# Ten products of a tuned decoder kernel moved from VectorE to GpSimd, six of them behind a ScalarE copy out of PSUM

## The chip, the cores and the metric

The kernel runs on one core of a Trainium2 chip. The metric is the device time of one execution in microseconds. The kernel before took 2746.87 us (median of 3 runs, 2746.59 to 2746.87). The engines are TensorE (PE in the profile), its weight loads (PEld), VectorE (DVE), ScalarE (ACT), GpSimd (POOL) and SyncE (SP), which here only issues loads.

## What is computed

The reference is a decoder trunk of two layers on 512 positions of width 2048: a pooling mixer (layer 0) and a gated linear recurrence (layer 1), each followed by a gated input embedding. The change lies in the first steps of layer 0:

```python
h = rmsnorm(x, g_pre[0])               # x * rsqrt(mean(x*x) + eps) * g
uz = jnp.einsum('bsd,de->bse', h, w_in[0])
u, z = uz[..., :D_INNER], uz[..., D_INNER:]
```

The product has 8192 output channels, 64 tiles of 128 channels by 512 positions. Tiles 0 to 31 are u, tiles 32 to 63 are z. All arithmetic is fp32.

## The kernel before

Activations lie with channels on the partitions and positions along the free axis, so a tile is 128x512. Each fp32 operand is split into a rounded part `hi` and a rest `lo`, and a product is three matmuls, hi by hi, hi by lo and lo by hi (`mm3`, lines 125 to 128). ScalarE makes `hi` and VectorE makes `lo`. For weights that is `chunk_of` (lines 100 to 123): SyncE loads a chunk into `raw`, ScalarE scales it by the gain into `hi` (L118), VectorE subtracts into `lo` (L119); `raw`, `hi` and `lo` have two buffers each.

The norm's factor for each position, `R`, is not known when the first product starts. So the product is taken of the raw x, and each result tile is multiplied by `R` afterwards. The order of the work is:

1. `first_unit` (line 228, written out by hand) makes tiles 0 to 3 of the product while x is still being loaded, and gathers the squares of x. It has four PSUM banks.
2. `raw_copies` (line 295) has ScalarE copy these four banks to SBUF (tiles zs0 to zs3). `norm.finish` (line 188) makes `R` in SBUF: ScalarE's square root, VectorE's reciprocal.
3. Lines 648 to 650: VectorE multiplies each of the four tiles by `R` in place (L649), and `keep` (line 336) stores it to DRAM, by a DMA that GpSimd's queue issues (L338). The stored u is read back much later, by `pool_in` (line 429).
4. Line 651: `unit` (line 130) makes tiles 4 to 9, with six PSUM banks of the eight, from 16 chunks. A chunk holds one of the 16 tiles of x's channels and 6 weight tiles: 18 matmuls of 512 columns.
5. Lines 652 to 659: `mix` and `renew` prepare sums and differences of x for the steps that follow; nearly all of it is VectorE's, with ScalarE's `hi` halves (L149) and VectorE's `lo` halves (L150) of `split`. `mix` also multiplies x by `R` (L347).
6. Lines 660 to 664: VectorE multiplies each of the six banks by `R` into an SBUF tile `u` (L663), and `keep` stores it. The tiles take turns in the tags D and F, two buffers each, so the fifth reuses the first's and the sixth the second's, once they are stored.
7. Lines 665 to 668: `pair_unit` (line 397) makes the other tiles, two at a time, with four banks, from four pair chunks (`pair_chunk`, line 368). A pair chunk needs on VectorE four sums of 128x256 (L384 to L387), the `lo` of three weight blocks (L388, 128x768) and two `lo` of sums (L150), and on ScalarE the `hi` of L382 and two of L149. With its weights TensorE does 42 matmuls of 256 columns (L410 to L412). The sums of even pair chunks are split into the slots zs0 to zs3. The finished pair leaves PSUM by VectorE (L415 to L422), and `keep` stores it.

Outside `first_unit` and the tail, the framework orders the instructions of each engine when the kernel is built, by priority and by its own estimate of when things are ready. What lies in `urgent()` has high priority: the chunks, the copies of `raw_copies`, and L663. At run time each engine goes through its queue in order, so an instruction that waits holds up what is behind it. GpSimd's queue holds the stores of `keep` in the order of their tiles, with little else between 2 us and the pools.

Of the kernel before, what the change touches and what calls it, by code (L numbers as in the profile page):

```python
# [10 lines left out]
ALU = mybir.AluOpType  # L11
# [31 lines left out]
def trunk(ctx: ExitStack, tc: tile.TileContext, order, xT, pT, wst, par, out):  # L43

    nc = tc.nc
    V, A, G, T = nc.vector, nc.scalar, nc.gpsimd, nc.tensor
# [8 lines left out]
    def bank(name):  # L55
        return ps.tile([P, S], F32, tag="bank", name=name)
# [3 lines left out]
    def tmp(tag, name):  # L60
        return work.tile([P, S], F32, tag=tag, name=name, bufs=BUFS[tag])

    def urgent(now=True):
        return tc.high_priority() if now else nullcontext()
# [65 lines left out]
    def unit(kind, layer, xs, kts, ets, trickle=False, gain=True):  # L130


        ne, nk = len(ets), len(kts)
        banks = [bank(f"{kind}_{e}") for e in range(ne)]
        per = CH // ne
        cuts = list(range(0, nk, per))
        for a, b in zip(cuts, cuts[1:] + [nk]):
            ks = range(a, b)
            hi, lo = ahead.pop(0) if ahead else chunk(kind, layer, [kts[k] for k in ks], ets, gain)
            steps = [(k, e) for e in range(ne) for k in ks]  # L140
            if trickle and ks[-1] < nk - 1:
                steps.sort()
            for k, e in steps:
                t = (k - a) * ne + e
                mm3(banks[e], hi[:, t, :], lo[:, t, :], *xs[k], k == 0, k == nk - 1)
        return banks
# [148 lines left out]
    def raw_copies(banks, tags):  # L295

        r = []
        for b, t in zip(banks, tags):
            c = slot(t, F32, "rawc")
            with urgent():  # L300
                A.copy(c, b)
            r.append(c)
        return r
# [32 lines left out]
    def keep(m, t):  # L336

        G.dma_start((U + Z)[m], t)  # L338
# [307 lines left out]
    b = raw_copies(b0, [f"zs{e}" for e in range(4)])  # L646
    R = norm.finish()
    for e in range(4):
        V.tensor_tensor(b[e], b[e], R, op=ALU.mult)  # L649
        keep(e, b[e])  # L650
    b = unit("w_in", 0, X, KX, range(4, 10))
    for kk in range(6):
# [7 lines left out]
    for e in range(6):  # L660
        t = tmp("DF"[e % 2], "u")
        with urgent():
            V.tensor_tensor(t, b[e], R, op=ALU.mult)  # L663
        keep(4 + e, t)
    for m in range(10, 60, 2):
        pair_unit(m)
# [2 lines left out]
    b = unit("w_in", 0, X, KX, range(60, 64), gain=False)  # L669
    ds = pool_in(0)  # L670
    zs = gate_in(0)
    for e in range(4):
        t = tmp("F", "z")
# [40 lines left out]
    for k in range(NK):  # L714
        t = es[k]
# [5 lines left out]
    b = unit("w_in", 1, X, KX, [0, 1, 2, 3, 32], trickle=True)  # L721
    b = raw_copies(b, ["c8", "c10", "c12", "c14", "zs0"])
    R = norm.finish()
# [6 lines left out]
    for n in range(1, NU):  # L730
        b = unit("w_in", 1, X, KX, range(4 * n, 4 * n + 4))
# [25 lines left out]
    b = [bank("w_ple_gate_h") for _ in range(2)]  # L757
# [9 lines left out]
    with tc.manual_schedule():  # L767
        b = [bank("w_ple_gate_h") for _ in range(2)]
# [38 lines left out]
        for k in range(8):  # L807
# [3 lines left out]
            b = held[k // 2]  # L811
# [68 lines left out]
```

## Time and profile before

| What | us |
|---|---|
| median of 3 runs | 2746.87 |
| the profiled execution, its own time | 2747.97 |
| its span, first to last instruction | 2746.3 |
| TensorE busy | 2734.5 |
| VectorE busy | 2007.7 |
| ScalarE busy | 1185.4 |
| GpSimd busy | 148.7 |

The span is 1.7 us shorter than the same execution's time. A matmul's end is modelled, and matmuls overlap, so TensorE's busy share tells only where it stood still. Times within the span count from its first instruction. In a timeline each line gives the start, the time taken, engine, line, operation, out<-in and the number of instructions merged in it, and in brackets the idle time before it and what ended that.

### The profile page before, as it was taken

To read this page: it belongs to the slowest core of one execution; us is meant where nothing else is said; L and a number is where in the kernel's file an instruction comes from. 1 tells how busy PE (TensorE), PEld (TensorE's weight loads), DVE (VectorE), ACT (ScalarE), POOL (GpSimd) and SP (SyncE) were. 2 spreads that over 40 slices of the span, in tenths; PEclk is the share of its full clock that TensorE was granted. 3 is DMA by queue.
4 is the path that set the end of the run, shared out by engine and by line. 5 is a ranking of instruction groups with operands and counts; after the bars stand their busy time and mean duration, and the time that the engine had idled before them with its cause. 6 is when DMAs were issued, how large, how long until landed. Compare 5 with 4: busy or idle time off the path is not lost.

```text
span 2746.3 us, 36706 instructions
## 1 busy us (share of the span) xinstructions
PE 2734.5 (100%) x14124; PEld 2350.5 (86%) x14124; DVE 2007.7 (73%) x3219; ACT 1185.4 (43%) x1731; POOL 148.7 (5%) x265
## 2 busy tenths in 40 slices
PE   9999999999999999999999999999999999999999
PEld 8899999998888888888888888888888888888887
DVE  6988888788848554577488876767686858598856
ACT  6444444444423222255365543434343434345554
POOL 0000000014303000000000000000000000000002
PEclk9999999999999999999999999999999999999999
DMA  5334434346534333333323233233233332332333
GB/s 179 124 124 136 134 127 135 124 142 219 161 115 142 119 112 104 115 117 95 104 85 107 92 100 99 93 100 97 96 100 93 99 97 95 100 101 92 96 94 117
DMA packets 98576, 314.57 MB, mean 115 GB/s; under 512 B 12000, under 2 KB 16224, under 8 KB 98400
## 3 DMA queue, kind: packets, MB, share of 16 engines
q1 hardware_dynamic: 84384, 271.58, 31.4%
q0 software_dynamic: 11200, 36.71, 3.9%
q10 hardware_dynamic: 2816, 3.94, 0.4%
q8 instruction: 110, 1.80, 0.3%
q14 instruction: 66, 0.54, 0.1%
HBM read 291.21 MB, written 20.97 MB: 114 GB/s over the span
## 4 chain that ended last, share of the span: by engine, by line
PE 98%; DVE 1%; DMA 0%; issue 0%; ACT 0%; ACTq 0%; DVEq 0%
PE w_in L128 10%; PE w_in L126 10%; PE w_in L127 10%; PE w_out L128 8%; PE w_out L126 8%; PE w_out L127 8%; PE w_in_s L412 6%; PE w_in_s L410 6%; PE w_in_s L411 6%; PE w_ple_gate L127 4%; PE w_ple_gate L128 4%; PE w_ple_gate L126 4%; PE pool_w L128 2%; PE pool_w L126 2%; PE pool_w L127 2%; PE w_in L264 2%
## 5 line engine op out<-in xcount | busy, mean ns | idle before, releaser
L119 DVE SCALAR_TENSOR_TENSOR lo<-raw,pr,hi 128x512 fp32r<-128x512 f32 (+5 forms) x424 | 290.5, 718 | 319.9 <-ACT hi L118 310.9
L118 ACT ACTIVATE hi<-raw,pr 128x512 fp32r<-128x512 f32 (+5 forms) x424 | 277.5, 696 | 449.4 <-PE w_in L127 273.6
L126 PE MATMUL w_in<-xhi,hi 128*128 128x512 f32 x1184 | 461.5, 390 | 0.0
L127 PE MATMUL w_in<-xlo,hi 128*128 128x512 f32 x1184 | 460.6, 389 | 0.0
L128 PE MATMUL w_in<-xhi,lo 128*128 128x512 f32 x1184 | 460.3, 389 | 0.0
L128 PE MATMUL w_out<-yhi,lo 128*128 128x512 f32 x1024 | 398.7, 389 | 0.0
L126 PE MATMUL w_out<-yhi,hi 128*128 128x512 f32 x1024 | 398.4, 389 | 0.0
L127 PE MATMUL w_out<-ylo,hi 128*128 128x512 f32 x1024 | 398.4, 389 | 0.0
L122 DVE TENSOR_TENSOR lo<-raw,hi 128x1024 fp32r<-128x1024 f32 (+2 forms) x194 | 234.2, 1207 | 213.4 <-ACT hi L121 207.6
L121 ACT ACTIVATE hi<-raw 128x1024 fp32r<-128x1024 f32 (+2 forms) x194 | 203.7, 1050 | 424.8 <-PE w_out L127 232.8
L126 PEld LDWEIGHTS w_in<-xhi,hi 128*128 128x128 f32 x1184 | 222.2, 188 | 46.8 <-ACT ig L512 0.3
L127 PEld LDWEIGHTS w_in<-xlo,hi 128*128 128x128 f32 x1184 | 222.2, 188 | 46.7 <-issue 0.5
L128 PEld LDWEIGHTS w_in<-xhi,lo 128*128 128x128 f32 x1184 | 222.2, 188 | 46.1 <-DVE lo L119 0.2
L128 PEld LDWEIGHTS w_out<-yhi,lo 128*128 128x128 f32 x1024 | 192.2, 188 | 40.9 <-DVE lo L122 1.0
L127 PEld LDWEIGHTS w_out<-ylo,hi 128*128 128x128 f32 x1024 | 192.2, 188 | 40.0
L126 PEld LDWEIGHTS w_out<-yhi,hi 128*128 128x128 f32 x1024 | 192.2, 188 | 39.7
L126 PE MATMUL w_ple_gate<-xhi,hi 128*128 128x512 f32 x480 | 187.4, 391 | 0.0
L128 PE MATMUL w_ple_gate<-xhi,lo 128*128 128x512 f32 x480 | 186.8, 389 | 0.0
L127 PE MATMUL w_ple_gate<-xlo,hi 128*128 128x512 f32 x480 | 186.7, 389 | 0.0
L315 DVE TENSOR_TENSOR o<-w_out,o 128x512 f32<-128x512 f32 x224 | 152.0, 684 | 33.2 <-PE w_out L128 31.4
L382 ACT ACTIVATE hi<-raw 128x768 fp32r<-128x768 f32 x100 | 84.7, 847 | 150.9 <-PE w_in_s L411 143.9
L149 ACT ACTIVATE s24hi<-s 128x512 fp32r<-128x512 f32 x100 | 63.2, 632 | 130.2 <-PE w_in_s L411 113.4
(283 smaller groups left out, 5525.5 us busy)
## 6 DMA issues: line engine op xcount, KB each, us to landing
raw<-in_w SPq DMA_DIRECT2D x420, 512.0 KB, 3.5
raw<-in_w SPq DMA_DIRECT2D x60, 384.0 KB, 3.0
raw<-in_w SPq DMA_DIRECT2D x48, 320.0 KB, 2.9
u<-u POOLq DMA_DIRECT2D x38, 256.0 KB, 3.5
zs<-z POOLq DMA_DIRECT2D x32, 256.0 KB, 4.0
z<-pair POOLq DMA_DIRECT2D x28, 256.0 KB, 3.0
u<-pair POOLq DMA_DIRECT2D x22, 256.0 KB, 3.0
raw<-in_w SPq DMA_DIRECT2D x17, 256.0 KB, 5.4
```

The lines of the kernel that those rows point to most:

```text
L118: A.activation(hi[:, sl, :], raw[:, sl, :], AF.Copy, scale=g)
L119: V.scalar_tensor_tensor(lo[:, sl, :], raw[:, sl, :], g, hi[:, sl, :].bitcast(F32), op0=ALU.mult, op1=ALU.subtract)
L121: A.activation(hi, raw, AF.Copy)
L122: V.tensor_tensor(lo, raw, hi.bitcast(F32), op=ALU.subtract)
L126: T.matmul(acc, hi, xhi, start=start, stop=False)
L127: T.matmul(acc, hi, xlo, start=False, stop=False)
L128: T.matmul(acc, lo, xhi, start=False, stop=stop)
L315: V.tensor_tensor(O[k], banks[e], O[k], op=ALU.add)
L382: A.activation(hi, flat[:, H:], AF.Copy)
L410: T.matmul(acc[p], hi, x[0][:, ts], start=kk == 0 and p in (1, 6, 3, 4), stop=False, skip_group_check=True)
L411: T.matmul(acc[p], hi, x[1][:, ts], start=False, stop=False, skip_group_check=True)
L412: T.matmul(acc[p], lo, x[0][:, ts], start=False, stop=kk == NK // 2 - 1, skip_group_check=True)
```

## The change

VectorE's products with `R` in lines 649 and 663 become GpSimd's. [...] Each product stands ahead of its own store, which GpSimd's queue issues too. The copy and the product of the six are both urgent; the first four products are not, as before.

```diff
@@ -646,7 +646,7 @@
     b = raw_copies(b0, [f"zs{e}" for e in range(4)])
     R = norm.finish()
     for e in range(4):
-        V.tensor_tensor(b[e], b[e], R, op=ALU.mult)
+        G.tensor_tensor(b[e], b[e], R, op=ALU.mult)
         keep(e, b[e])
     b = unit("w_in", 0, X, KX, range(4, 10))
     for kk in range(6):
@@ -660,7 +660,8 @@
     for e in range(6):
         t = tmp("DF"[e % 2], "u")
         with urgent():
-            V.tensor_tensor(t, b[e], R, op=ALU.mult)
+            A.copy(t, b[e])
+            G.tensor_tensor(t, t, R, op=ALU.mult)
         keep(4 + e, t)
     for m in range(10, 60, 2):
         pair_unit(m)
```

## Rows read from the trace of the kernel before

**Rows 1.** The page: busy time, share of the span and instructions of each engine.

```profile
PE 2734.5 (100%) x14124; PEld 2350.5 (86%) x14124; DVE 2007.7 (73%) x3219; ACT 1185.4 (43%) x1731; POOL 148.7 (5%) x265
```

**Rows 2.** Waits of TensorE over the span: us in total, times, longest.

```profile
PE w_in_s L412 <- DVE lo L388: 3.5, 1, 3.5
```

**Rows 3.** Timeline of TensorE, 117 to 130 us: start, us, engine, line, operation.

```profile
117.67 0.28 PE L410 MATMUL w_in_s<-xhi,hi 128*128 128x256 f32 x1
...
120.66 0.28 PE L411 MATMUL w_in_s<-t34lo,hi 128*128 128x256 f32 x1
124.39 0.39 PE L412 MATMUL w_in_s<-xhi,lo 128*128 128x256 f32 x1 [3.45 <-DVE lo L388]
...
125.57 0.36 PE L411 MATMUL w_in_s<-xlo,hi 128*128 128x256 f32 x1
...
129.11 0.28 PE L412 MATMUL w_in_s<-xhi,s24lo 128*128 128x256 f32 x1
129.23 0.28 PE L410 MATMUL w_in_s<-t12hi,s13hi 128*128 128x256 f32 x1
```

**Rows 4.** Stretches: length, busy PE, PEld, DVE, ACT, POOL, granted clock, DMA share, GB/s.

```profile
122.00:124.00 2.00, 0.00 (x0) 0.00 (x0) 2.00 (x5) 0.63 (x1) 1.08 (x2) 1.00 0.50 191
126.00:128.00 2.00, 2.00 (x11) 2.00 (x11) 2.00 (x5) 0.00 (x1) 0.00 (x0) 0.50 0.55 215
```

**Rows 5.** Timelines of VectorE and ScalarE, 113 to 125 us.

```profile
113.29 0.42 DVE L384 TENSOR_TENSOR s<-raw 128x256 f32<-128x256 f32 x1 [0.80 <-DMA raw<-in_w]
...
116.64 2.47 DVE L663 TENSOR_TENSOR u<-w_in,R_pre 128x512 f32<-128x512 f32 x4
...
121.14 1.33 DVE L663 TENSOR_TENSOR u<-w_in,R_pre 128x512 f32<-128x512 f32 x2 [1.02 <-DMA u<-u]
...
123.39 1.82 DVE L388 TENSOR_TENSOR lo<-raw,hi 128x768 fp32r<-128x768 f32 x2
...
117.69 0.85 ACT L382 ACTIVATE hi<-raw 128x768 fp32r<-128x768 f32 x1 [1.19 <-issue]
...
120.51 0.84 ACT L382 ACTIVATE hi<-raw 128x768 fp32r<-128x768 f32 x1
```

**Rows 6.** Timelines of VectorE and TensorE, 58 to 94 us.

```profile
58.40 2.49 DVE L649 TENSOR_TENSOR rawc<-rawc,R_pre 128x512 f32<-128x512 f32 x4
...
65.71 1.02 DVE L119 SCALAR_TENSOR_TENSOR lo<-raw,pr,hi 128x768 fp32r<-128x768 f32 x1
...
69.16 0.39 PE L128 MATMUL w_in<-xhi,lo 128*128 128x512 f32 x1
...
91.19 1.01 DVE L119 SCALAR_TENSOR_TENSOR lo<-raw,pr,hi 128x768 fp32r<-128x768 f32 x1
...
93.64 0.39 PE L128 MATMUL w_in<-xhi,lo 128*128 128x512 f32 x1
```

**Rows 7.** Stretches 58 to 113 and 113 to 125 us, columns as in rows 4.

```profile
58.00:113.00 55.00, 55.00 (x244) 45.53 (x244) 54.50 (x97) 28.52 (x43) 2.33 (x4) 1.00 0.38 116
113.00:125.00 12.00, 8.55 (x53) 7.52 (x52) 10.65 (x23) 5.88 (x9) 3.24 (x6) 1.00 0.59 215
```

**Rows 8.** Instructions of line 301: ns min/median/max, first and last start, forms.

```profile
L301 ACT COPY rawc<-w_in x9: 564/588/607, 51.6 to 1460.1; 128x512 f32<-128x512 f32 x9
```

**Rows 9.** Instructions of line 338, and us from issue to landing.

```profile
L338 POOL DMA_DIRECT2D u<-u x6: 539/539/544, 117.6 to 122.8; - x6
...
DMA to landing us min/median/max: 2.3/3.2/5.6
```

**Rows 10.** Timeline of GpSimd in the tail.

```profile
2735.96 4.84 POOL L780 TENSOR_TENSOR rawc<-rawc,o 128x256 f32<-128x256 f32 x7 [1.17 <-DVE rawc L777]
```

**Rows 11.** Instructions of lines 627 and 622, one of each beside GpSimd's sums of L780.

```profile
L627 DVE TENSOR_TENSOR nacc_out<-nacc_out,gsg x2: 426/708/989, 2717.1 to 2726.0; 128x256 f32<-128x256 f32 x2
...
L622 DVE TENSOR_TENSOR sq_last<-rawc x2: 424/626/828, 2718.4 to 2731.3; 128x256 f32<-128x256 f32 x2
```

**Rows 12.** Instructions of line 456, GpSimd's copies in the pools.

```profile
L456 POOL COPY s<-s x48: 183/661/3449, 652.5 to 887.5; 128x2 f32<-128x2 f32 x24, 128x4 f32<-128x4 f32 x16, 128x8 f32<-128x8 f32 x8
```

## The prediction

> **What bounds the kernel now.** I read the page's busy shares first: TensorE is busy 2734.5 us of the span [rows 1]. So the change can matter only where TensorE waits, and the view of who waited for whom, kept to TensorE, lists all of that. The line to see is the longest: one wait of 3.5 us, matmul L412 on VectorE's lo of L388 [rows 2]. The four others, each shorter, lie at the very start and end of the span, where this change does nothing. Between this wait and the tail there is none, so a changed order of later work has nothing to win there.
>
> Next I read what that one wait costs. The matmul before it started at 120.66, it started at 124.39, and such matmuls normally start 0.12 apart (129.11 and 129.23): 3.61 us lost [rows 3]. [...] From 125.57 to 129.11 there are 17 steps from start to start in 3.54 us, where 17 x 0.12 = 2.04 would do: 1.50 us lost. The hole costs 3.61 + 1.50 = 5.1 us, and that is all that can be gained here.
>
> Then why lo is late: VectorE's timeline. It prepares the first pair chunk from 113.29, then does four of the six products with R (L663, from 116.64), the sums of the next chunk, and stands 1.02 us in front of the fifth product, whose tile is still being stored. Only then comes the awaited lo, at 123.39 [rows 5]. The six products and the wait are 6 x 0.60 + 1.0 = 4.6 us right ahead of the late instruction. The change aims at a real hole.
>
> **The change part by part.**
>
> Removed from VectorE: ten products. Four take 2.47 us from 116.64 [rows 5] and four 2.49 from 58.40 [rows 6], about 0.6 each as they overlap: 10 x 0.60 = 6.0 us, and the 1.02 us wait. Between 58 and 113 us VectorE is busy 54.5 of 55.0 us [rows 7], so 2.4 us less there moves everything behind it forward; TensorE does not wait there, so nothing is gained from it directly. The 3.6 + 1.0 us at 116 to 121 are worth up to the whole hole.
>
> Added on ScalarE: six copies out of PSUM, 0.59 us each by the same form elsewhere (L301) [rows 8]: 3.5 us. In 113 to 125 us ScalarE is busy 5.9 of 12.0 us [rows 7], so they fit. The fifth and sixth copy reuse the tiles of the first and second, so on ScalarE's queue they stand in front of the next hi until those are stored. The pair's matmuls begin at 117.67 [rows 3], right behind the last chunk's 18, which are 0.227 apart (108 of them lie between the two matmuls of rows 6, 24.48 us); the first bank's three are the first of them, done near 114.5, and its copy ends near 115.1; a product (below) takes 1.4, the store's issue 0.54, its landing 3.2 to 5.6 [rows 9]: near 120.3 for the first, 1.9 later for the second, so ScalarE may stand until 122.2. Behind it waits the hi of the third pair chunk, at 120.51 before [rows 5]; at 123 with its lo by 125 it is still ahead of 127.7, when TensorE gets there (117.67 + 2 x 42 x 0.12). Cost nothing; if a store landed 3 us later it would begin to cost.
>
> Added on GpSimd: ten products of 128x512. No row has one. The nearest is the sum of two 128x256 tiles at the end: seven in 4.84 us, 0.69 apart [rows 10]. For twice the columns the bounds are 0.69 and 1.38; I take 1.38, as the work is per column. The six products and stores take turns in one queue: 6 x (1.38 + 0.54) = 11.5 us from 115, done by about 127; the first four by 67, the last landing near 70, while their tiles are next written after the sums of 113.29 [rows 5]. Nobody reads what is stored before the pools, which come after all pair units. So GpSimd being slower costs nothing by itself.
>
> What it does to VectorE is the term that decides. VectorE's 128x256 instructions with two inputs in SBUF run 0.43 us undisturbed and 0.99 (L627) and 0.83 (L622) beside GpSimd's sums, a loss of 0.56 and 0.40 [rows 11]. In return GpSimd's copies of two to eight columns, 0.18 us at their shortest, have a median of 0.66 us where VectorE is busy, and one took 3.4 [rows 12]. So each holds the other up. For a 128x512 product I take a loss to VectorE of 2 x 0.56 = 1.12 us; bounds 0 (the product always falls into a gap of VectorE's) and 1.38 (its whole length). Nearly all VectorE work here has two SBUF inputs, and without gaps in it the product always displaces something. [...]
>
> So each product frees 0.60 us of VectorE and takes about 1.12.
>
> First stretch: the four products put VectorE 4 x 1.12 = 4.5 us behind by about 67. What waits is TensorE, for lo (L119): the one started at 65.71, 1.02 long, is used at 69.16, a margin of 2.4 us; the tightest, at 91.19, is used at 93.64, a margin of 1.4 [rows 6]. TensorE stands 4.5 - 2.4 = 2.1 us (0 to 4.1 by the bounds). The 2.4 us that VectorE is relieved of lie behind this point and help later.
>
> Second stretch: the hi of the second chunk runs from 117.69 to 118.54 [rows 5], its lo could end by 119.5, and TensorE needs it at 117.67 + 42 x 0.12 = 122.7: a margin of 3.2 us. Four products fit in before that (1.92 each from 115): 4.5 - 3.2 = 1.3 us of standing (0 to 5.1, with all six at 1.38).
>
> Clock: the one hole inside the kernel lost 1.50 us to the slow clock after 3.6 us of idling. Two short holes may bring none or 1.50 each; I take 0.75 in all.
>
> Sum: -5.1 + 2.1 + 1.3 + 0.75 = -0.95 us. The profiled execution took 2747.97 us (span 2746.3), 1.1 above the median of 2746.87; the difference applies alike: 2746.87 - 0.95 = 2745.9 us. A measurement of this kernel can tell about 0.2%, 5.5 us, from no change.
>
> **The rivals.**
>
> 1. The hole closes and nothing opens: GpSimd's products find gaps, or VectorE's margins hold. For it: 1.4 to 3.2 us of margin, and the 2.4 us relieved. Against it: no gap in 58 to 113. It gives 2746.87 - 5.1 = 2741.8 us, just short of 0.2%. Anything further would need time that TensorE doesn't lose today.
>
> 2. Slower: VectorE is held for the full 1.38 us of every product, and each is met by the tightest margin. First stretch 4 x 1.38 - 1.4 = 4.1, second 6 x 1.38 - 3.2 = 5.1, slow clock twice 1.50: 12.2 - 5.1 = +7.1, 2754.0 us. It passes +5.5 from a hold of about 1.22 us (10 x 1.22 - 4.6 + 3.0 - 5.1). For it: the losses on L627 and L622 are near their maximum. [...]
>
> 3. ScalarE's fifth and sixth copy wait for stores that GpSimd issues late. With each of GpSimd's first two products delayed by 3.4 us, as its worst copy was, the second store lands near 129, the third chunk's lo ends near 131.4 where TensorE wants it at 127.7: 3.7 us and 1.50 of clock, -5.1 + 5.2, 2747.0 us. For it: the queue is in order. Against it: the median wait is far shorter.
>
> **How the numbers follow.** The forecast, a hole partly given back: 0.50. Rival 1: 0.28, of which 0.06 beyond -5.5 us. Rival 2: 0.15. Rival 3: 0.07. Faster 0.06, same 0.79, slower 0.15. The range runs from rival 1 with a little to spare, 2741.4, up towards rival 2, 2752.5, which leaves out most of it.
>
> **What would show it.** TensorE's wait on L388 near 121 should be gone or under 2 us. A wait on L119 between 65 and 95 shows the first stretch right; none shows the hold smaller than I took, or hidden. VectorE's 128x512 instructions of 0.68 us beside the products should show 1.2 to 2 us. If they don't, the term that decides is wrong, and rival 1 stands. GpSimd's products should start about 1.9 us apart. A long wait of ScalarE on a store means rival 3. If TensorE stands over 10 us between 58 and 140, rival 2 is right.

## The result, and the profile after

The changed kernel took 2765.9 us (median of 4 runs, 2763.47 to 2769.64) beside 2746.87 for the kernel before: 1.007 times as long, 95% interval 1.0057 to 1.0082. It is slower by 0.7%, outside the range I gave. The profiled execution took 2763.47 us with a span of 2761.7, 15.4 us longer than the span before.

TensorE's waits come first, as before. Waits of TensorE over the changed kernel's span (us in total, times, longest):

```profile
PE w_in_s L412 <- DVE s13lo L150: 3.8, 8, 1.0
PE w_in_s L410 <- ACT hi L382: 3.4, 1, 3.4
PE w_in L128 <- DVE lo L119: 2.8, 1, 2.8
...
PE w_in_s L412 <- DVE lo L388: 0.2, 1, 0.2
```

The old hole [rows 2] is gone: L388 is down to 0.2 us. Three things stand in its place. One is a wait on L119, as the first stretch forecast, one a wait on ScalarE's hi of L382, and one is a kind that no step of the prediction has: eight waits on s13lo, seven of them after 160 us, where TensorE never stood before. The stretches around the first two (columns as in rows 4) show a granted clock of 0.50 again behind each, as in the second line of [rows 4]:

```profile
64.00:66.00 2.00, 0.00 (x0) 0.00 (x0) 2.00 (x5) 1.21 (x3) 0.49 (x1) 1.00 0.70 260
...
68.00:70.00 2.00, 2.00 (x6) 1.51 (x6) 2.00 (x6) 0.63 (x1) 0.00 (x0) 0.50 0.35 138
...
126.00:128.00 2.00, 0.00 (x0) 0.00 (x0) 2.00 (x5) 0.09 (x1) 2.00 (x4) 1.00 0.15 55
...
132.00:134.00 2.00, 2.00 (x11) 2.00 (x11) 2.00 (x3) 0.00 (x0) 1.68 (x3) 0.50 0.84 328
```

VectorE is busy in all four, 2.00 of 2.00 us, so the question is with what. Timeline of VectorE in the changed kernel:

```profile
56.73 3.49 DVE L347 SCALAR_TENSOR_TENSOR x<-x,pr,R_pre 128x512 f32<-128x512 f32 x2
60.14 3.58 DVE L350 TENSOR_TENSOR t<-x 128x256 f32<-128x256 f32 x1
...
120.74 1.51 DVE L384 TENSOR_TENSOR s<-raw 128x256 f32<-128x256 f32 x1
122.18 0.41 DVE L387 TENSOR_TENSOR s<-raw 128x256 f32<-128x256 f32 x1
122.51 4.43 DVE L385 TENSOR_TENSOR s<-s,raw 128x256 f32<-128x256 f32 x1
...
130.18 1.50 DVE L384 TENSOR_TENSOR s<-raw 128x256 f32<-128x256 f32 x1
...
131.94 1.94 DVE L385 TENSOR_TENSOR s<-s,raw 128x256 f32<-128x256 f32 x1
```

All but the first row are 128x256 instructions, which take 0.42 us in [rows 5]; here one takes 4.43. Beside them, GpSimd's timeline of the same kernel:

```profile
56.06 3.62 POOL L649 TENSOR_TENSOR rawc<-rawc,R_pre 128x512 f32<-128x512 f32 x2 [54.30 <-DVE R_pre L196]
...
60.89 2.54 POOL L649 TENSOR_TENSOR rawc<-rawc,R_pre 128x512 f32<-128x512 f32 x2
...
120.38 1.59 POOL L664 TENSOR_TENSOR u<-u,R_pre 128x512 f32<-128x512 f32 x1 [55.89 <-ACT u L663]
...
122.87 3.78 POOL L664 TENSOR_TENSOR u<-u,R_pre 128x512 f32<-128x512 f32 x3
...
129.83 1.57 POOL L664 TENSOR_TENSOR u<-u,R_pre 128x512 f32<-128x512 f32 x1 [1.59 <-ACT u L663]
...
132.30 1.29 POOL L664 TENSOR_TENSOR u<-u,R_pre 128x512 f32<-128x512 f32 x1
```

Each long 128x256 instruction ends about 0.3 us after GpSimd's product or products do. L385 at 122.51 ends at 126.94, three products from 122.87 end at 126.65: VectorE got no turn between them. Why the planner put two and three products in a row, with the stores behind them, the runs do not show. Nor do the starts tell which engine came first: L350 at 60.14 and L385 at 122.51 begin 0.75 and 0.36 us before the products that hold them, and GpSimd's times in a profile are rough. What VectorE lost in all: L347 3.49 - 1.41 (the pair's time without a product, shown further down) = 2.1; L350 3.2; then 1.1, 4.0, 1.1 and 1.5. That is 13.0 us for ten products, 1.3 each.

Where the time went along the span can be read from one instruction that every pair unit has once, the first of its evacuation (L415: count, ns, first and last start). In the kernel before:

```profile
L415 DVE COPY pairs<-w_in_s x25: 412/417/425, 140.1 to 623.8; 128x256 f32<-128x256 f32 x25
```

and in the changed kernel:

```profile
L415 DVE COPY pairs<-w_in_s x25: 417/419/425, 147.8 to 637.7; 128x256 f32<-128x256 f32 x25
```

The first is 7.7 us later, the last 13.9: the 24 units between them take 489.9 us instead of 483.7, with no product of the change anywhere near. So there are two losses, and the second can't be the products' presence itself. The split is rough, because TensorE began the chunks of `unit` at 51.97 us in the one execution and at 50.30 in the other. By the starts of TensorE's own matmuls, the changed kernel loses 6.3 us from there to the second pair, and 9.2 from there to the end of the pair units.

What differs in the pair units is the order that the planner gave VectorE. In the kernel before, with the evacuation under way (timeline of VectorE):

```profile
365.76 0.41 DVE L417 TENSOR_TENSOR pairs<-pairs,w_in_s 128x256 f32<-128x256 f32 x1
366.09 0.68 DVE L150 TENSOR_TENSOR s13lo<-s,s13hi 128x512 fp32r<-128x512 f32 x1
366.69 0.41 DVE L418 TENSOR_TENSOR pairs<-pairs,w_in_s 128x256 f32<-128x256 f32 x1
```

and in the changed kernel, at the same place of a unit:

```profile
378.81 0.41 DVE L417 TENSOR_TENSOR pairs<-pairs,w_in_s 128x256 f32<-128x256 f32 x1
...
379.48 0.42 DVE L418 TENSOR_TENSOR pairs<-pairs,w_in_s 128x256 f32<-128x256 f32 x1
...
381.47 0.95 DVE L388 TENSOR_TENSOR lo<-raw,hi 128x768 fp32r<-128x768 f32 x1
382.34 0.42 DVE L422 TENSOR_TENSOR pair<-pairs,w_in_s 128x256 f32<-128x256 f32 x1
382.67 0.69 DVE L150 TENSOR_TENSOR s13lo<-s,s13hi 128x512 fp32r<-128x512 f32 x1
383.27 0.69 DVE L150 TENSOR_TENSOR s24lo<-s,s24hi 128x512 fp32r<-128x512 f32 x1
```

There, s13lo stands behind the first three of the evacuation's eight instructions (L415 to L417); here behind all of it, three sums (L386, L384 and L387, among the lines left out) and an L388. TensorE's timeline of the changed kernel shows what that costs in this unit:

```profile
383.41 0.38 PE L412 MATMUL w_in_s<-t12hi,s13lo 128*128 128x256 f32 x1 [1.05 <-DVE s13lo L150]
```

The view of waits lists only the longer ones. By the starts of the matmul records, a matmul on s13lo begins more than 0.17 us behind the one ahead of it, where 0.12 is usual, 18 times after 160 us in the changed kernel, 6.7 us in all, and never in the kernel before.

The order repeats: of the 25 units, 22 have the same early order in the kernel before, and 24 the same late one in the changed kernel. I call them the **early** and the **late order**.

### The profile page after: what moved, and what is told of

Read it like the earlier page. It is cut to its first block, busy times and chain, and to the rows that moved or that the text cites. A ratio compares the mean times of both kernels' runs of the same rounds, so it can differ in the third digit from the quotient of the medians.

```text
span 2761.7 us, 36691 instructions
## 1 busy us (share of the span) xinstructions
PE 2741.9 (99%) x14124; PEld 2352.8 (85%) x14124; DVE 2011.4 (73%) x3209; ACT 1183.9 (43%) x1737; POOL 162.5 (6%) x275
## 4 chain that ended last, share of the span: by engine, by line
PE 88%; DVE 6%; DMA 4%; issue 1%; ACT 0%; POOL 0%; DVEq 0%; ACTq 0%; POOLq 0%
PE w_in L128 9%; PE w_in L126 9%; PE w_in L127 9%; PE w_out L126 8%; PE w_out L128 8%; PE w_out L127 8%; PE w_ple_gate L128 4%; PE w_ple_gate L126 4%; PE w_ple_gate L127 4%; DMA raw<-in_w 4%; PE w_in_s L412 4%; PE w_in_s L411 3%; PE w_in_s L410 3%; PE pool_w L128 2%; PE pool_w L127 2%; PE pool_w L126 2%
## 5 line engine op out<-in xcount | busy, mean ns | idle before, releaser
L119 DVE SCALAR_TENSOR_TENSOR lo<-raw,pr,hi 128x512 fp32r<-128x512 f32 (+5 forms) x424 | 290.8, 719 | 319.5 <-ACT hi L118 310.6
L382 ACT ACTIVATE hi<-raw 128x768 fp32r<-128x768 f32 x100 | 84.6, 846 | 137.0 <-PE w_in_s L411 119.1
```

Source lines behind the costliest of these rows:

```text
L119: V.scalar_tensor_tensor(lo[:, sl, :], raw[:, sl, :], g, hi[:, sl, :].bitcast(F32), op0=ALU.mult, op1=ALU.subtract)
L382: A.activation(hi, flat[:, H:], AF.Copy)
```

## The experiments

Two theories for the later loss. A, which the second batch calls C: the planner's order of the pair units is a loss of its own. B: all of it follows from GpSimd's hold on VectorE. A third question, D, is what the hold itself is. Each batch of four ran beside its own runs of the kernel before, whose medians were 2750.25, 2749.18 and 2752.12 us, spread over 9.6 to 11 us; so the ratios with their intervals count. The two columns on the right are first and last start of L415 in the profiled execution.

| run | GpSimd's products | order | median, us | ratio to before, interval | first, last L415 |
|---|---|---|---|---|---|
| four | first 4 | late | 2762.13 | 1.0042 (1.0027 to 1.0057) | 141.0, 635.4 |
| six | last 6 | early | 2750.81 | 1.0002 (0.9993 to 1.0012) | 143.8, 629.2 |
| copy | none | late | 2757.93 | 1.0023 (1.0012 to 1.0033) | 138.8, 633.0 |
| half | 10, half width | early | 2750.79 | 0.9998 (0.9988 to 1.0008) | 142.0, 625.7 |
| before_tag | none | late | 2759.76 | 1.0032 (1.0020 to 1.0044) | 140.6, 635.9 |
| after_tag | 10 | early | 2754.79 | 1.0018 (1.0008 to 1.0028) | 147.8, 630.4 |
| copy_mix | none | early | 2748.53 | 0.9992 (0.9982 to 1.0001) | 139.5, 623.2 |
| copy_order | none | early | 2745.80 | 0.9985 (0.9976 to 0.9995) | 136.8, 622.0 |
| tag_set | 10 fills | early | 2743.00 | 0.9968 (0.9958 to 0.9978) | 135.0, 619.9 |
| tag_one | 10, one input | early | 2747.93 | 0.9987 (0.9977 to 0.9998) | 141.1, 621.2 |
| four_tag | first 4 | early | 2753.29 | 1.0005 (0.9994 to 1.0016) | 145.3, 628.7 |
| after_again | 10 | late | 2767.12 | 1.0060 (1.0036 to 1.0083) | 149.7, 642.0 |

### One part alone: four, six, copy, half

four: the kernel before with

```diff
     for e in range(4):
-        V.tensor_tensor(b[e], b[e], R, op=ALU.mult)
+        G.tensor_tensor(b[e], b[e], R, op=ALU.mult)
```

> Only the first four products on GpSimd; the six stay on VectorE, without a copy. Theory A (two separate costs: GpSimd's products hold VectorE for their whole length, and the planner's new order of the pair units, which comes with the six copies, loses about 10 us later): the order of the pair units is close to that of before, so only the first stretch is paid: VectorE instructions of about 3.5 us near 57 to 63, a wait of TensorE on L119 near 66 of about 2.8 us with its slow clock, the old hole on L388 still there, and no growth after 160 us. 2749 to 2753 us. Theory B (all 19 us follow from the hold, the later drift being VectorE's lag that is never made up): 4 of 10 products, some 2754 us, with small waits of TensorE on s13lo all through the pair units.

six: the kernel before with

```diff
         with urgent():
-            V.tensor_tensor(t, b[e], R, op=ALU.mult)
+            A.copy(t, b[e])
+            G.tensor_tensor(t, t, R, op=ALU.mult)
```

> Only the six products on GpSimd, behind their ScalarE copies; the first four stay on VectorE. Theory A: the pair units have the new order (TensorE's is the same as in the changed kernel), so the later drift of about 10 us is there, and the wait in the first stretch (2.8 us and its slow clock) is gone: 2760 to 2763 us. Theory B: 6 of 10 products, 2746.9 + 11 = 2758 us.

copy: the same, with `V.tensor_tensor(t, t, R, op=ALU.mult)` for the product.

> The six copies on ScalarE as in the change, but all ten products on VectorE, the six from the SBUF copy; no GpSimd product at all. Theory A: the pair units stand in nearly the order of the changed kernel, so the drift of about 10 us after 160 us is there without any hold, and TensorE waits on s13lo: 2752 to 2759 us. Theory B: no product on GpSimd, no hold, no drift: 2742 to 2748 us.

half: the changed kernel with both products on `[:, :S // 2]` of their tiles.

> The changed kernel with each GpSimd product on the first 256 of 512 columns; the other 256 columns of these ten tiles are left unscaled. TensorE's order is the same. If the hold is the length of the product, the long VectorE instructions shrink to about half (4.43 us for three products to about 2.4, 3.5 for two to about 2), and the waits of 2.8 us on L119 and 3.4 us on ScalarE's hi nearly go: about 6 to 8 us less than the changed kernel. Theory A: the drift after 160 us stays, 2757 to 2760 us. Theory B: the drift halves too, near 2756 us, with about 5 us of growth after 160. If the hold does not depend on length, the time stays at 2764 to 2766 us.

Three of the four missed both theories' numbers: four is far above, six far below, and half 5 us below the nearer one. I had tied the late order to the copies, and that was wrong. Read by the order that each kernel in fact got, the runs fall apart cleanly: in the late order the 24 steps of L415 take 494.4 us (four) and 494.2 (copy), in the early one 485.4 (six) and 483.7 (half). copy has no product on GpSimd and grows as much as four, which B can't have. half fits a hold that goes with the length of the product. Its GpSimd timeline shows two products of 256 columns in a row:

```profile
122.62 1.43 POOL L664 TENSOR_TENSOR u<-u,R_pre 128x256 f32<-128x256 f32 x2
```

and its VectorE timeline the instruction that they hold, 1.81 us, where three of 512 columns held one for 4.43, so 0.70 lost for each product instead of 1.34:

```profile
122.54 1.81 DVE L386 TENSOR_TENSOR s<-raw,s 128x256 f32<-128x256 f32 x1
```

half also has the early order, so its distance to the changed kernel, 0.7%, is not the hold's alone. The order had to be set apart.

### The order alone: before_tag, after_tag, copy_mix, copy_order

before_tag is the kernel before, after_tag the changed kernel, both with the same letter changed, the fifth tile's tag:

```diff
-        t = tmp("DF"[e % 2], "u")
+        t = tmp("DFDFFF"[e], "u")
```

> The kernel before with one letter changed: the fifth of the six tiles takes the tag F instead of D. All ten products stay on VectorE, no copies. The planner then settles on the other order of VectorE's work in 22 pair units, the one that the changed kernel has: the awaited lo of L388 and the sums of the next chunk stand ahead of the pair's evacuation, and two s13lo late. Theory C (the planner's order of the pair units is a loss of its own, about 0.4 to 0.5 us a unit, whatever led to it): TensorE waits on s13lo, growth of 8 to 13 us after 160 us, 2756 to 2762 us. Theory B (the later drift follows from GpSimd's hold): no hold, no drift, 2747 to 2752 us.

> The changed kernel with the same one letter: all ten products on GpSimd, copies as in the change. Here the letter sends the planner back to the order of the pair units of before. Theory C: the growth after 160 us falls to that of the runs in that order (2 to 6 us), while the waits near 66 and 130 us from GpSimd's products stay: 2750 to 2757 us, 9 to 15 below the changed kernel. Theory B: the ten holds are all there, so 2763 to 2769 us.

copy_mix is copy with

```diff
     mix(6)
+    renew(4)
     mix(7)
-    for kk in range(4, 8):
+    for kk in range(5, 8):
         renew(kk)
```

> Six copies on ScalarE, all ten products on VectorE, and one preparation step (renew(4)) moved ahead of mix(7), which sends the planner to the order of the pair units of before. Theory C: no hold, no late order, and the old hole on L388 closed (the copy kernel was 3.3 us ahead of before at 130 us): 2743 to 2749 us, below the kernel before by 1 to 5 us. Theory B has nothing to hold here either, but gave copy no drift, so it does not expect a gain over the 2757.9 us of copy.

copy_order is copy with

```diff
-    for e in range(6):
+    for e in (0, 1, 2, 5, 4, 3):
```

> As copy (six copies on ScalarE, all products on VectorE), with the six taken in the order 0, 1, 2, 5, 4, 3, which also sends the planner to the order of the pair units of before. Theory C: 2743 to 2751 us, some 8 to 13 below copy; its first pair unit differs, so its start may lose a little more or less than copy_mix. Rival (the drift belongs to the copies themselves): as copy, 2756 to 2759 us.

Theory C's numbers came in all four. The letter makes the kernel before 0.32% slower, without a product moved. TensorE's waits of before_tag from 160 to 640 us, a list that is empty for the kernel before:

```profile
PE w_in_s L412 <- DVE s13lo L150: 6.6, 10, 1.9
```

Its L415 line:

```profile
L415 DVE COPY pairs<-w_in_s x25: 411/416/425, 140.6 to 635.9; 128x256 f32<-128x256 f32 x25
```

It starts level with the kernel before (140.6) and ends 12.1 us behind. The same letter takes the changed kernel from 1.0060 to 1.0070 down to 1.0018, with the products and their holds all there; L415 in after_tag:

```profile
L415 DVE COPY pairs<-w_in_s x25: 412/417/425, 147.8 to 630.4; 128x256 f32<-128x256 f32 x25
```

It starts where the changed kernel does, 147.8, and takes 482.6 us for the 24 steps instead of 489.9. So the two losses are apart: the order is worth 0.42 to 0.52% by the medians, some 12 to 14 us (10.0 us between the spans of the two profiled executions), and the products 0.18%, 5 to 6 us, against the kernel before with its hole. Between these two kernels TensorE's instructions stand in the same order; VectorE's and ScalarE's differ. What TensorE loses is at s13lo, VectorE's: a matmul on it is late 18 to 23 times after 160 us in every run with the late order, 6.7 to 9.8 us in all, and never in one with the early order.

copy_order comes out below both kernels, by a little against the kernel before: 0.9985 (0.9976 to 0.9995), all products on VectorE and only the copies on ScalarE. Its waits of TensorE in the pair units are one of 1.2 us on L388 and one of 0.3, so the hole shrinks without closing. VectorE's products take as long as before, 1.29 us for two in SBUF; the 1.02 us that VectorE stood for a store in [rows 5] are ScalarE's here, 0.86 us. How much of the gain that is, and how much the new places of the products, was not set apart. copy_mix, 0.9992 (0.9982 to 1.0001), is not told from the kernel before.

### The hold alone: tag_set, tag_one, four_tag, after_again

tag_set is after_tag with

```diff
-        G.tensor_tensor(b[e], b[e], R, op=ALU.mult)
+        G.memset(b[e], 1.0)
...
-            G.tensor_tensor(t, t, R, op=ALU.mult)
+            G.memset(t, 1.0)
```

> after_tag with each of GpSimd's ten products replaced by a fill of the same tile: it writes 512 columns and reads nothing (the ten tiles are filled with ones, so their scaled product is left out). The orders of TensorE, VectorE and ScalarE are the same instruction for instruction as in after_tag. Theory D (VectorE's instructions with two SBUF inputs and GpSimd's that read SBUF hold each other up for a whole instruction): nothing is held, no VectorE instruction of 1.5 to 4.5 us, the waits of 2.8 us near 66 and near 130 us are gone: 2743 to 2748 us, 7 to 11 below after_tag. Rival (VectorE is late because of what waits for GpSimd's slow chain, the stores and ScalarE's copies behind them, or because any GpSimd work beside it slows it): the copies and stores are still there, so at least half of the two waits stays, 2750 to 2755 us.

tag_one has `G.tensor_scalar(t, t, 1.5, None, op0=ALU.mult)` in these places.

> after_tag with each of GpSimd's ten products replaced by one with a constant in place of R: one SBUF input instead of two (R's factor is left out of the ten tiles). The orders of TensorE, VectorE and ScalarE are again those of after_tag. Theory D: reading one tile is enough to hold VectorE, for as long as it takes; if that is 0.5 to 0.8 us, VectorE instructions are lengthened by that, by 1.5 to 2.5 us where three stand in a row, and most of the two waits goes: 2745 to 2751 us. Rival (only two inputs on GpSimd's side collide): as tag_set, with no lengthened instruction.

four_tag is four with the letter of before_tag.

> The first four products on GpSimd, the six on VectorE without copies (the kernel four), with the one letter that sends the planner to the order of the pair units of before. Theory C: the growth of four after 160 us (13 us) goes, and what stays is the wait near 66 us of about 2.8 us with its slow clock, while the old hole on L388 may or may not stay: 2748 to 2754 us, 8 to 13 below four. Theory B: 2760 to 2763 us, as four.

> The changed kernel once more, on the chip of the three runs beside it, so that its distance from the kernel before can be read from the same set: both theories expect 2762 to 2770 us.

tag_set is the cleanest test here, since TensorE, VectorE and ScalarE run the same instructions in the same order as in after_tag. By the ratios it falls 0.5% below after_tag, to 0.9968. VectorE's timeline in tag_set, the places that took 3.49, 3.58 and 4.43 us in the changed kernel, and what runs beside three fills:

```profile
56.36 1.41 DVE L347 SCALAR_TENSOR_TENSOR x<-x,pr,R_pre 128x512 f32<-128x512 f32 x2
57.69 0.42 DVE L350 TENSOR_TENSOR t<-x 128x256 f32<-128x256 f32 x1
...
116.07 0.69 DVE L150 TENSOR_TENSOR xlo<-x,xhi 128x512 fp32r<-128x512 f32 x1
116.67 0.42 DVE L386 TENSOR_TENSOR s<-raw,s 128x256 f32<-128x256 f32 x1
...
117.16 0.69 DVE L150 TENSOR_TENSOR s13lo<-s,s13hi 128x512 fp32r<-128x512 f32 x1
...
120.07 0.42 DVE L385 TENSOR_TENSOR s<-s,raw 128x256 f32<-128x256 f32 x1
```

and GpSimd's, with three fills in a row as there were three products:

```profile
116.03 1.47 POOL L664 MEMSET u<- 128x512 f32 x3
```

The fills come earlier against VectorE than the products did, and are shorter, 0.5 us each. The first four are over by 54 us, before VectorE's work at 56.36, so the test rests on the other six; none of VectorE's instructions beside these is lengthened. The fills, which only write, do not hold VectorE here: three instructions beside the row of three take 0.69, 0.42 and 0.69 us. The products, which read two tiles, do: one instruction takes 4.43 us beside three of them.

tag_one, with one input, came within its range, but not by the mechanism I expected. GpSimd's timeline:

```profile
119.06 4.94 POOL L664 TENSOR_SCALAR u<-u 128x512 f32<-128x512 f32 x3
```

and VectorE's in the same time:

```profile
118.73 1.25 DVE L386 TENSOR_TENSOR s<-raw,s 128x256 f32<-128x256 f32 x1
...
120.00 0.68 DVE L150 TENSOR_TENSOR s13lo<-s,s13hi 128x512 fp32r<-128x512 f32 x1
120.67 1.03 DVE L150 TENSOR_TENSOR s24lo<-s,s24hi 128x512 fp32r<-128x512 f32 x1
...
121.70 0.95 DVE L388 TENSOR_TENSOR lo<-raw,hi 128x768 fp32r<-128x768 f32 x1
122.57 0.82 DVE L384 TENSOR_TENSOR s<-raw 128x256 f32<-128x256 f32 x1
```

Three of VectorE's two-input instructions in this time are lengthened, by 0.35 to 0.83 us; those between them take their usual 0.68 and 0.95. GpSimd's take 1.65 us each, longer than the products with two inputs (1.26 in the row of three) and than the 0.5 to 0.8 us that I had supposed. So VectorE gets through while a GpSimd instruction of this kind still runs. A hold for the whole instruction fits the products (4.43 us beside three of 3.78 in all) and not these; why the two kinds differ was not tried further, nor what becomes of VectorE's instructions with one input.

four_tag has the wait on L119 (2.8 us) and no growth (483.4 us for the 24 steps, where four had 494.4): 1.0005 for 1.0042. after_again repeats the result, 1.0060.

## Why the prediction was wrong

**What bounds the kernel**: the hole, its place and cause were right. L388's wait went from 3.5 to 0.2 us. The 5.1 us that I gave as all that the hole can return are nearly what tag_set shows, with all ten products off VectorE and fills in their place on GpSimd: from the first matmul of `unit` to the second pair, TensorE takes 5.2 us less there than in the kernel before. Its median is 9.1 us below its own runs of the kernel before (2743.00 and 2752.12); the other 4 us have no cause that the runs show.

**"A changed order of later work has nothing to win there"** is the sentence that failed. It is true and I stopped at it. It has something to lose: one edit near the start can make the planner order all later work anew, the pair units then repeat one order 22 to 24 times, and the late order costs 0.3 to 0.5 us a unit. The sum had no term for it, and there was no rival for it. It made the larger part of the loss, 0.42 to 0.52%.

**The loss of VectorE per product**, the term I said decides, was mis-sized: 1.12 us taken, 1.3 measured (13.0 for ten), nearly the bound of 1.38. The spacing was wrong too. I had GpSimd's products 1.9 us apart with a store between; two and three came in a row, and VectorE got no turn between them, so 4 us were lost at once. Whether the same holds, spread out, would have cost TensorE less is not shown.

**First stretch**: 2.1 us of standing forecast, 2.8 measured, on the line named but a chunk earlier. The matmul that waited, at 66.37, needs the lo of the fourth chunk, which began at 61.50 in the kernel before; I had taken the fifth's, at 65.71. VectorE in the kernel before, right behind the four products of [rows 6]:

```profile
60.81 0.74 DVE L347 SCALAR_TENSOR_TENSOR x<-x,pr,R_pre 128x512 f32<-128x512 f32 x1
61.50 1.02 DVE L119 SCALAR_TENSOR_TENSOR lo<-raw,pr,hi 128x768 fp32r<-128x768 f32 x1
```

In the changed kernel seven of `mix`'s instructions stand ahead of this lo, which begins at 65.31. So the 2.4 us that VectorE was relieved of did not "help later": the planner had filled them.

**Second stretch**: 1.3 forecast, 3.4 and 0.2 measured. The instruction that waited was not lo but hi. VectorE's held sum (L385) stood ahead of L386, on which ScalarE's s24hi waited, and the next hi of L382 stood behind that. ScalarE in the changed kernel:

```profile
127.91 0.63 ACT L149 ACTIVATE s24hi<-s 128x512 fp32r<-128x512 f32 x1 [4.65 <-DVE s L386]
128.44 0.83 ACT L382 ACTIVATE hi<-raw 128x768 fp32r<-128x768 f32 x1
```

I followed VectorE's own lo and not what waits for VectorE on ScalarE.

**Clock**: 0.75 us taken for both holes, some 4.8 lost, of the sum's terms for the products the one furthest off. The granted clock fell to 0.50 behind both, as after the old hole [rows 4], and TensorE's steps grew to 0.43 us from 0.227 behind the first and to 0.21 from 0.12 behind the second. TensorE in the changed kernel:

```profile
66.37 0.50 PE L128 MATMUL w_in<-xhi,lo 128*128 128x512 f32 x1 [2.81 <-DVE lo L119]
...
71.05 0.39 PE L126 MATMUL w_in<-xhi,hi 128*128 128x512 f32 x1
...
129.32 0.58 PE L410 MATMUL w_in_s<-xhi,hi 128*128 128x256 f32 x1 [3.39 <-ACT hi L382]
...
135.81 0.28 PE L410 MATMUL w_in_s<-t34hi,s13hi 128*128 128x256 f32 x1
```

From 66.37 to 71.05 there are 13 steps, where 13 x 0.227 = 2.95 us would do: 1.73 lost. From 129.32 to 135.81 there are 27, where 27 x 0.12 = 3.24 would do: 3.25 lost, 0.2 of it the wait on L388. With what was measured the prediction's own sum becomes -5.1 + 2.8 + 3.6 + 4.8 = +6.1 us, beside the 6.3 that TensorE loses up to the second pair. So the first part is accounted for, and the rest is the 9.2 us of the pair units.

**Rival 2** had the mechanism and nearly the price for the products alone: +7.1 us given, +5.6 measured between the medians of after_tag and before. That the sums are so near is partly luck: it gave 9.2 us of standing and 3.0 of slow clock, and the changed kernel has 6.4 and 4.8. It got 0.15 and I kept the forecast on its better side. **Rival 3** did not happen: ScalarE's fifth and sixth copies were not what TensorE waited for. **Rival 1** is what tag_set shows, with no reading by GpSimd, and copy_order in part. The range missed for want of the order: even rival 2's price in full, 2754.0, is 11.9 us below what was measured.

## What to carry to other kernels

Before an elementwise product goes to GpSimd, look at what VectorE does at that time: beside instructions with two SBUF inputs and no gaps, each product here took from VectorE more than it had cost there, 1.3 us for 0.6. Copying the banks out by ScalarE and leaving the products on VectorE was 0.15% better than the kernel before in one order (copy_order), no different in another (copy_mix) and 0.23% worse in the late one (copy), so the order decided more than the copies. And where a planner orders the work, compare the order of the repeated part before believing any cause for a small difference: one letter in a tag was worth 0.3% the wrong way here.

## What was not expected of the hardware

GpSimd's products in a row held one VectorE instruction for all of them, 4.43 us for three, while its one-input instructions in a row (4.94 us for three) let VectorE's through, with 0.35 to 0.83 us added to three of them. Three fills of 128x512 in a row, which read nothing, added nothing: 0.42 and 0.69 us beside them, as without.
